# Memory keys and cross-attention queries of an encoder block: two heads at once, high half of the weights with both halves of the activations in one matmul

## The chip, the cores and the metric

The kernel runs on one core of a Trainium2 chip. The metric is the device time in microseconds of one launch; three runs of the kernel before gave 1122.85, 1123.02 and 1123.64 us. Engines: TensorE (PE; its weight loads PEld), VectorE (DVE), ScalarE (ACT), GpSimd (POOL) and SyncE (SP), which here issues the transfers.

## The reference

One encoder block in float32, 256 tokens of width 2048. A mixer of two attention groups is followed by LN1; then cross-attention over 256 memory tokens with four heads of 128, LN2, and an MLP with squared ReLU, LN3. The part that matters here:

```
def memory_cross_attention(h, mem_n, w_q_mem, w_kv_mem, w_o_mem):
    q = (h @ w_q_mem).reshape(b, s, MEM_HEADS, MEM_HEAD_DIM)
    kv = (mem_n @ w_kv_mem).reshape(b, m, 2, MEM_HEADS, MEM_HEAD_DIM)
    k, v = kv[:, :, 0], kv[:, :, 1]
    scores = jnp.einsum('bqhd,bmhd->bhqm', q, k) * (MEM_HEAD_DIM ** -0.5)
    probs = jax.nn.softmax(scores, axis=-1)
    o = jnp.einsum('bhqm,bmhd->bqhd', probs, v).reshape(b, s, MEM_WIDTH)
    return o @ w_o_mem

    x = layer_norm(ALPHA * x + mix, ln1_g[l], ln1_b[l])
    mem_n = layer_norm(mem, mem_ln_g[l], mem_ln_b[l])
    xa = memory_cross_attention(x, mem_n, w_q_mem[l], w_kv_mem[l], w_o_mem[l])
    x = layer_norm(ALPHA * x + xa, ln2_g[l], ln2_b[l])
```

## The kernel before, in words

Every float32 factor is held as a high and a low part (`split`, lines 77 to 84: ScalarE rounds the high part, VectorE subtracts it from the source for the low one). A product is the sum of three matmuls: high by high, high by low, low by high. Activations stand transposed, one block of 128 rows of the contraction beside the next, each as 256 columns of high parts and 256 of low parts.

Weights come as 1 MB transfers into one of three raw buffers (`Stream.next`, line 121). Each raw tile makes two pairs `w_hi`, `w_lo` of 1024 columns, and there are four such pairs. A raw buffer is free again when VectorE has made the second low part from it. A pool of seven temporaries of 512 columns (`tmp_tile`) serves the layer norms, the softmax and the gains and biases; four PSUM banks (`acc`) hold the projections, four more (`att`) the transposes and scores.

In the stage at hand, from 292 us on, TensorE computes for each of four heads the memory keys `km` (`mem_k`, line 613; 16 blocks of 128 rows, `cols_mm`, lines 183 to 187: three matmuls of 256 columns for a block), then the queries `qm` from the normalized activations `x1t` (`mem_q`, line 644; two heads per call), scores and softmax of heads in turn (`softmax`, line 322), the memory values `vm` (line 677, eight halves of weights from four loads, 12 matmuls of 512 columns for a half), the probabilities times values (`values`) and the output projection `w_om`. Beside the keys, the pieces of LN1 are done: `x1t` is transposed on TensorE (line 534, `turn`), scaled on ScalarE (line 542), split on both. Beside the queries the residual gets LN1's gains and biases: `residual` loads a row of 512 values of `ln1_g` or `ln1_b`, broadcast to all partitions, into a temporary (line 561), and VectorE multiplies or adds it to the two blocks of the residual (line 565). After that four halves of the first MLP weights are prepared in a large tile `wide_0` (line 668) from two loads of `w_mi`.

The order of instructions on each engine is chosen by a scheduler from the program's dependences at build time; on the chip each engine then works strictly in that order. Loads share SP's one queue.

The MLP uses `cols_wide` (line 189): for several accumulators of 512 columns, the high weights meet the 512 columns of both activation halves in one matmul, and the low weights meet the 256 high columns in another; `hidden` (line 706) later adds the two halves of the accumulator.

Of the kernel before, what the change touches and what calls it, by code (L numbers as in the profile page):

```python
# [14 lines left out]
AF = mybir.ActivationFunctionType  # L15
ALU = mybir.AluOpType
AX = mybir.AxisListType

P = 128
S = 256  # L20
D = 2048
KT = D // P
# [4 lines left out]
HM = 4  # L27
# [4 lines left out]
SC_A = float(DH) ** -0.5  # L32
# [6 lines left out]
def encoder_kernel(ctx: ExitStack, tc: tile.TileContext, t, out):  # L39
    nc = tc.nc  # L40
# [18 lines left out]
    def f(ap):  # L59
        return ap.bitcast(F32)  # L60

    def acc_tile():
        return psA.tile([P, 512], F32, tag="acc", name="acc")
# [10 lines left out]
    def pin(ins, pinned):  # L74
        return tc.keep_in_program_order(ins) if pinned else ins

    def split(hi, lo, src, scale=None, pinned=False):
        if scale is None:
            pin(nc.scalar.activation(hi, src, AF.Copy), pinned)  # L79
            return pin(nc.vector.tensor_tensor(out=lo, in0=src, in1=f(hi), op=ALU.subtract), pinned)  # L80
        else:
            nc.scalar.activation(hi, src, AF.Copy, scale=scale)
            nc.vector.scalar_tensor_tensor(
                out=lo, in0=src, scalar=scale, in1=f(hi), op0=ALU.mult, op1=ALU.subtract)
# [11 lines left out]
    def pump(n=1):  # L96

        for _ in range(n):
            if side:
                side.popleft()()  # L100
# [82 lines left out]
    def cols_mm(ps, hi, lo, xt, k, nk):  # L183

        nc.tensor.matmul(ps, hi, xt[:, k, 0:S], start=k == 0, stop=False)  # L185
        nc.tensor.matmul(ps, hi, xt[:, k, S:2 * S], start=False, stop=False)  # L186
        nc.tensor.matmul(ps, lo, xt[:, k, 0:S], start=False, stop=k == nk - 1)  # L187
# [244 lines left out]
    ps = proj_tokens(Stream(t["w_ka"]), xt, KT, KVA * DH)  # L432
# [3 lines left out]
    ps = proj_tokens(Stream(t["w_vkr"]), xt, KT, KVA * DH + ROPE)  # L436
    for b in range(NB):
# [3 lines left out]
        a, c, e = krn[:, 0:64], krn[:, 64:128], krn[:, 256:512]  # L441
        nc.vector.tensor_tensor(out=a, in0=v, in1=krt[:, 0, b, :], op=ALU.mult)
        for i in range(2):
            j = 1 - i
            nc.vector.tensor_tensor(out=c[:, i * 32:(i + 1) * 32], in0=v[:, j * 32:(j + 1) * 32],
                                    in1=krt[:, 1, b, i * 32:(i + 1) * 32], op=ALU.mult)
        nc.gpsimd.memset(e, 0.0)
        for par in range(2):
            dst = e[:, par * P:(par + 1) * P].rearrange("p (i g c) -> p i g c", g=2, c=32)
            nc.vector.tensor_tensor(  # L450
                out=dst[:, :, par, :], in0=a.rearrange("p (i c) -> p i c", c=32),
                in1=c.rearrange("p (i c) -> p i c", c=32), op=ALU.add)
# [25 lines left out]
    for n in range(2):  # L478
        ps = proj_tokens(s_vb, ckv, RANK // P, 512)
# [97 lines left out]
    def big3(name):  # L577
        return big.tile([P, 8192], F32R, tag="big", name=name).rearrange("p (k c) -> p k c", c=512)
# [17 lines left out]
    memt = big3("memt")  # L596
# [13 lines left out]
    km = midp.tile([P, 2048], F32R, tag="mid", name="km").rearrange("p (h c) -> p h c", c=512)  # L610
    s_km = Stream(t["w_km"])

    def mem_k(h):
        ps = acc_tile()[:, :S]
        for half in range(2):
            hi, lo = s_km.next()
            for j in range(8):
                c = slice(j * P, (j + 1) * P)
                cols_mm(ps, hi[:, c], lo[:, c], memt, half * 8 + j, KT)
        split(km[:, h, 0:S], km[:, h, S:2 * S], ps)  # L620

    x1t = big3("x1t")
    side.extend(norm_transposed(res_chunk, sts, 1, x1t))
# [4 lines left out]
    qm = attC[:, 2048:4096].rearrange("p (h c) -> p h c", c=512)  # L628
    om = attC[:, 4096:6144].rearrange("p (h c) -> p h c", c=512)

    def together(nexts, xt_, mm, outs):

        n = len(outs)
        for k in range(0, KT, 8 // n):
            hi, lo = nexts(k)
            for j in range(8 // n):
                for i in range(n):
                    c = slice((j * n + i) * P, (j * n + i + 1) * P)
                    mm(outs[i], hi[:, c], lo[:, c], xt_, k + j, KT)

    s_qm = Stream(t["w_qm"], beside=2)
    wide0 = []

    def mem_q(g):
        outs = [acc_tile()[:, :S] for _ in range(2)]
        together(lambda k: s_qm.next(), x1t, cols_mm, outs)
        for j in range(2):
            h = 2 * g + j
            split(qm[:, h, 0:S], qm[:, h, S:2 * S], outs[j], SC_A)

    def mem_scores(h):
        pt = attC[:, 6144 + (h - 2) * 1024:6144 + (h - 1) * 1024] if h >= 2 else None
# [4 lines left out]
               om, h)  # L657

    s_km.beside = 2
    for h in range(HM):  # L660
        mem_k(h)
    pump(len(side))
    side.extend(residual("ln1"))
    mem_q(0)
# [12 lines left out]
    ps = proj_tokens(Stream(t["w_vm"]), memt, KT, 512)  # L677
# [9 lines left out]
    for n in range(4):  # L687
        ps = proj_tokens(s_om, om, HM, 512, by_block=n == 3)
# [48 lines left out]
    for c in range(NCH):  # L737
# [7 lines left out]
        for n in range(4):  # L745
            tiles = att_tile if n >= 2 else acc_tile
            if c == NCH - 1 and n == 3:
                wide_w = [big.tile([P, 8192], F32R, tag="big", name=f"w{i}") for i in range(2)] + [None]
                ps = proj_tokens(None, ht, CH, 512, by_block=True, wide=last_weights, tiles=tiles)
            else:  # L750
                ps = proj_tokens(s_mo, ht, CH, 512, by_block=False, tiles=tiles)
# [13 lines left out]
    for b in range(NB):  # L765
# [10 lines left out]
        for i, c in enumerate(cols):  # L776
            if i + 1 < len(cols):
                shift(cols[i + 1])
            pin(nc.vector.scalar_tensor_tensor(
                out=res[b][:, c], in0=res[b][:, c], scalar=r, in1=b3[:, c],  # L780
# [4 lines left out]
def _rows(w, kt, cols):  # L785

    k, n = w.shape
    u = w.reshape(k // (kt * P), kt, P, n // cols, cols)
    return np.ascontiguousarray(u.transpose(3, 0, 2, 1, 4)).reshape(-1, P, kt * cols)
# [17 lines left out]
def _layout(i):  # L807
    f32 = np.float32
    a = {}
    x = np.asarray(i["x"])[0]  # L810
    a["x"] = x
    a["xT"] = np.ascontiguousarray(x.T.reshape(4, 4, P, S).transpose(0, 2, 1, 3)).reshape(4, P, 4 * S)
    a["mem"] = np.asarray(i["mem"])[0]
    w = np.asarray(i["w_in"])[0]
    qa, ka, va, cq, ckv, kr = np.split(w, np.cumsum([1024, 256, 256, 512, 512]), axis=1)
    a["w_qa"] = _rows(_pairs(qa, DH), 4, 512)
    a["w_ka"] = _rows(_pairs(ka, DH), 8, 256)
    a["w_vkr"] = _rows(np.concatenate([va, _pairs(kr, ROPE)], axis=1), 4, 320)
    a["w_cq"] = _rows(cq, 4, 512)
    a["w_ckv"] = _rows(ckv, 4, 512)  # L820
    gains = []
    for n in ("g_qa", "g_ka"):
        g = _pairs(np.asarray(i[n])[0], DH)
        gains += [g, g[DH // 2:], g[:DH // 2]]
    a["g_qk"] = np.concatenate(gains)
    a["g_cq"], a["g_ckv"] = np.asarray(i["g_cq"])[0], np.asarray(i["g_ckv"])[0]
    uq = np.asarray(i["w_uq"])[0].reshape(RANK, HB, DH + ROPE)
    ukv = np.asarray(i["w_ukv"])[0].reshape(RANK, HB, 2 * DH)

    def cols(m):  # L830
        return m.reshape(4, P, P).transpose(1, 0, 2).reshape(P, 512)
    halves = []
    for p in range(4):
        if p % 2 == 0:
            for pp in (p, p + 1):
                r = _pairs(uq[:, 2 * pp:2 * pp + 2, DH:], ROPE).reshape(RANK, 2, 2, 32)
                halves.append(cols(np.ascontiguousarray(r.transpose(0, 2, 1, 3)).reshape(RANK, P)))
        halves += [cols(uq[:, 2 * p + j, :DH]) for j in range(2)]
        halves += [cols(ukv[:, 2 * p + j, :DH]) for j in range(2)]
    a["w_b"] = np.ascontiguousarray(  # L840
        np.stack(halves).reshape(5, 4, P, 512).transpose(0, 2, 1, 3)).reshape(5, P, 2048)
    a["w_vb"] = _rows(np.ascontiguousarray(ukv[:, :, DH:]).reshape(RANK, HB * DH), 4, 512)
    wo = np.asarray(i["w_out"])[0]
    a["w_out"] = np.concatenate([_rows(wo[:1024], 4, 512), _rows(wo[1024:], 4, 512)])
    kv = np.asarray(i["w_kv_mem"])[0]
    a["w_km"] = _rows(kv[:, :512], 16, P)
    a["w_vm"] = _rows(kv[:, 512:], 4, 512)
    a["w_qm"] = _rows(np.asarray(i["w_q_mem"])[0], 8, 256)
    a["w_om"] = _rows(np.asarray(i["w_o_mem"])[0], 4, 512)
    mi = np.asarray(i["w_mlp_in"])[0]  # L850
    a["w_mi"] = _rows(mi, 4, 512)
    mo = np.asarray(i["w_mlp_out"])[0]
    a["w_mo"] = np.concatenate([_rows(mo[c * CH * P:(c + 1) * CH * P], 4, 512) for c in range(NCH)])
    for n in ("ln1", "ln2", "ln3", "mem_ln"):
        for s in "gb":
            a[f"{n}_{s}"] = np.asarray(i[f"{n}_{s}"])[0]

    a["norm_rows"] = np.ascontiguousarray(np.stack(
        [[a[f"{n}_{s}"].reshape(KT, P) for s in "gb"] for n in ("mem_ln", "ln1", "ln2")]
    ).transpose(3, 0, 1, 2))  # L860

    ang = _angles(DH)
    c, s = np.cos(ang).astype(f32), np.sin(ang).astype(f32)
    cc, ss = np.concatenate([c, c], 1), np.concatenate([-s, s], 1)

    def nat(m):
        return np.ascontiguousarray(m.reshape(NB, P, -1).transpose(1, 0, 2)).reshape(P, -1)
    a["rope_a"] = np.concatenate([nat(cc), nat(ss)], axis=1)
    ang = _angles(ROPE)
    c, s = np.cos(ang).astype(f32), np.sin(ang).astype(f32)  # L870
    cc, ss = np.concatenate([c, c], 1), np.concatenate([-s, s], 1)
    a["rope_kr"] = np.concatenate([nat(cc), nat(ss)], axis=1).reshape(P, 2, NB, ROPE)
    ct, st = c.T, s.T
    a["rope_qr"] = np.ascontiguousarray(
        np.stack([np.concatenate([ct] * 4), np.concatenate([-st, -st, st, st])], axis=1))
    a["rope_qr"] = (a["rope_qr"] * f32(SC_B)).astype(f32)
    return a
# [18 lines left out]
```

## Time and profile before

| | us |
|---|---|
| median of three runs | 1123.02 |
| profiled execution | 1123.25 |
| its span | 1121.4 |
| TensorE busy | 1105.5 (99%) |
| VectorE busy | 729.0 (65%) |
| ScalarE busy | 537.0 (48%) |

The profiled execution is one run with the hardware profiler; its span is the time from its first to its last instruction, and the mean granted clock of TensorE in it is 0.998 of full speed. Busy shares are averages over stages with different limits. A timeline row gives the start in microseconds from the start of the span, the duration, the engine, the line of the code, the operation and its tiles; a matmul's duration is longer than the distance to the next one, since they are pipelined, so their cost is read from starts. For waits, an arrow names who released the waiting instruction.

### The profile page before, as it was taken

What the parts mean: (1) busy time and instruction counts of PE and PEld (TensorE: products, weight loads), DVE (VectorE), ACT (ScalarE), POOL (GpSimd) and SP (SyncE); (2) the same over time, 40 slices, a digit from 0 to 9 for tenths busy, and PEclk for the clock granted to TensorE, in tenths of its full rate; (3) what the DMA queues carried; (4) which work ended last, traced back from release to release, by engine and by line L of the source; (5) the groups of instructions that cost most, each with busy time, mean ns of one, the idle gap of its engine ahead of it and who ended that gap; (6) DMA issues with size and microseconds to landing.
All of it is one profiled execution on the core that took longest, in us unless ns stands there. A gap on an engine that the chain in (4) does not pass through costs nothing.

```text
span 1121.4 us, 15079 instructions
## 1 busy us (share of the span) xinstructions
PE 1105.5 (99%) x6004; PEld 954.2 (85%) x6004; DVE 729.0 (65%) x1036; ACT 537.0 (48%) x778; POOL 38.2 (3%) x45
## 2 busy tenths in 40 slices
PE   9999999999999989999999999999999999999996
PEld 6988899888998878888888888888888888888885
DVE  5878677687788677854545565555556454665575
ACT  6555565546576344543344454334444333544440
POOL 1402000000100000000000000000000000000000
PEclk9999999999999999999999999999999999999999
DMA  9664454476467426655555555555555555555562
GB/s 336 224 225 151 150 188 150 151 240 239 162 224 262 150 75 225 204 205 193 188 189 189 188 186 192 195 198 177 208 188 188 193 188 188 188 188 188 191 259 76
DMA packets 37942, 215.85 MB, mean 192 GB/s; under 512 B 4336, under 2 KB 5232, under 8 KB 14192
## 3 DMA queue, kind: packets, MB, share of 16 engines
q1 hardware_dynamic: 37872, 214.89, 54.6%
q8 instruction: 47, 0.77, 0.3%
q14 instruction: 23, 0.19, 0.1%
HBM read 212.78 MB, written 2.10 MB: 192 GB/s over the span
## 4 chain that ended last, share of the span: by engine, by line
PE 96%; DMA 2%; DVE 1%; ACT 0%; issue 0%; SPq 0%; POOL 0%; DVEq 0%; ACTq 0%
PE acc L146 12%; PE acc L145 12%; PE acc L147 12%; PE acc L194 11%; PE att L194 11%; PE att L147 6%; PE att L145 6%; PE att L146 6%; PE acc L199 5%; PE att L199 5%; PE acc L187 2%; PE acc L185 2%; PE acc L186 2%; PE att L534 1%; PE att L349 1%; DMA raw<-in_w_ka 1%
## 5 line engine op out<-in xcount | busy, mean ns | idle before, releaser
L80 DVE TENSOR_TENSOR w_lo<-raw,w_hi 128x1024 fp32r<-128x1024 f32 (+2 forms) x374 | 444.6, 1193 | 327.4 <-ACT w_hi L79 326.3
L79 ACT ACTIVATE w_hi<-raw 128x1024 fp32r<-128x1024 f32 (+2 forms) x374 | 386.5, 1036 | 459.0 <-PE acc L147 171.0
L194 PE MATMUL att<-x2t,w_hi 128*128 128x512 f32 x512 | 139.6, 394 | 0.0
L194 PE MATMUL acc<-x2t,w_hi 128*128 128x512 f32 x480 | 130.9, 394 | 0.0
L145 PE MATMUL acc<-w_hi,ht 128*128 128x512 f32 x256 | 99.6, 389 | 0.0
L146 PE MATMUL acc<-w_lo,ht 128*128 128x512 f32 x256 | 99.6, 389 | 0.0
L147 PE MATMUL acc<-w_hi,ht 128*128 128x512 f32 x256 | 99.6, 389 | 0.0
L194 PEld LDWEIGHTS att<-x2t,w_hi 128*128 128x128 f32 x512 | 88.1, 189 | 12.3
L194 PEld LDWEIGHTS acc<-x2t,w_hi 128*128 128x128 f32 x480 | 82.5, 189 | 11.5
L146 PE MATMUL att<-w_lo,ht 128*128 128x512 f32 x224 | 87.1, 389 | 0.0
L147 PE MATMUL att<-w_hi,ht 128*128 128x512 f32 x224 | 87.1, 389 | 0.0
L145 PE MATMUL att<-w_hi,ht 128*128 128x512 f32 x224 | 87.0, 389 | 0.0
L199 PEld LDWEIGHTS att<-x2t,w_lo 128*128 128x128 f32 x512 | 77.5, 189 | 10.2
L199 PEld LDWEIGHTS acc<-x2t,w_lo 128*128 128x128 f32 x480 | 72.6, 189 | 9.5
L199 PE MATMUL att<-x2t,w_lo 128*128 128x256 f32 x512 | 80.2, 281 | 0.0
L199 PE MATMUL acc<-x2t,w_lo 128*128 128x256 f32 x480 | 75.1, 281 | 0.0
L146 PE MATMUL acc<-w_lo,xt 128*128 128x512 f32 (+2 forms) x192 | 69.5, 363 | 0.2 <-DVE w_lo L80 0.2
L147 PE MATMUL acc<-w_hi,xt 128*128 128x512 f32 (+2 forms) x192 | 69.1, 361 | 0.0
L145 PE MATMUL acc<-w_hi,xt 128*128 128x512 f32 (+2 forms) x192 | 66.1, 364 | 1.0 <-ACT w_hi L79 1.0
L147 PEld LDWEIGHTS acc<-w_hi,ht 128*128 128x128 f32 x256 | 48.0, 188 | 10.0
L145 PEld LDWEIGHTS acc<-w_hi,ht 128*128 128x128 f32 x256 | 48.0, 188 | 10.0
L146 PEld LDWEIGHTS acc<-w_lo,ht 128*128 128x128 f32 x256 | 48.0, 188 | 10.0
(221 smaller groups left out, 1738.1 us busy)
## 6 DMA issues: line engine op xcount, KB each, us to landing
raw<-in_w_mi SPq DMA_DIRECT2D x64, 1024.0 KB, 4.8
raw<-in_w_mo SPq DMA_DIRECT2D x64, 1024.0 KB, 4.8
raw<-in_w_out SPq DMA_DIRECT2D x16, 1024.0 KB, 4.9
raw<-in_w_b SPq DMA_DIRECT2D x5, 1024.0 KB, 4.8
raw<-in_w_qa SPq DMA_DIRECT2D x16, 256.0 KB, 5.4
raw<-in_w_qa SPq DMA_DIRECT2D x4, 1024.0 KB, 4.9
raw<-in_w_ckv SPq DMA_DIRECT2D x4, 1024.0 KB, 5.1
raw<-in_w_cq SPq DMA_DIRECT2D x4, 1024.0 KB, 4.8
```

What stands on the lines that cost most here:

```text
L79: pin(nc.scalar.activation(hi, src, AF.Copy), pinned)
L80: return pin(nc.vector.tensor_tensor(out=lo, in0=src, in1=f(hi), op=ALU.subtract), pinned)
L145: nc.tensor.matmul(ps, ah, bh, start=start, stop=False)
L146: nc.tensor.matmul(ps, ah, bl, start=False, stop=False)
L147: nc.tensor.matmul(ps, al, bh, start=False, stop=stop)
L185: nc.tensor.matmul(ps, hi, xt[:, k, 0:S], start=k == 0, stop=False)
L186: nc.tensor.matmul(ps, hi, xt[:, k, S:2 * S], start=False, stop=False)
L187: nc.tensor.matmul(ps, lo, xt[:, k, 0:S], start=False, stop=k == nk - 1)
L194: nc.tensor.matmul(ps, hi[:, i * P:(i + 1) * P], xt[:, k, :], start=k == 0, stop=k == nk - 1)
L199: nc.tensor.matmul(ps[:, 0:S], lo[:, i * P:(i + 1) * P], xt[:, k, 0:S], start=False, stop=False)
L349: nc.tensor.transpose(pp[:, st * S + b * P:st * S + b * P + P], ev[:, b, st * P:(st + 1) * P], ident)
L534: nc.tensor.transpose(ps[:, o:o + P], x(b, k // 4)[:, (k % 4 + j) * P:(k % 4 + j + 1) * P], ident)
```

## The change

The weights of the memory keys are laid out for two heads (256 columns of eight blocks in a raw tile instead of 128 columns of 16). Both `mem_k` and `mem_q` now take two heads and two accumulators of 512 columns, and call `cols_wide`: one matmul of 512 columns with the high weights and one of 256 with the low weights for a head and block, instead of three of 256. The new `halves_sum` then has ScalarE copy the second half of an accumulator into a temporary and VectorE add the first half to it; the split of keys or queries works on that sum instead of PSUM. `together` is gone. Below line 640 the new file's line numbers are 5 higher.

```diff
-    def mem_k(h):
-        ps = acc_tile()[:, :S]
-        for half in range(2):
+    def halves_sum(ps):
+
+        tt = tmp_tile()
+        lo, h = tt[:, 0:S], tt[:, S:2 * S]
+        nc.scalar.activation(lo, ps[:, S:2 * S], AF.Copy)
+        nc.vector.tensor_tensor(out=h, in0=ps[:, 0:S], in1=lo, op=ALU.add)
+        return h
+
+    def mem_k(g):
+
+        outs = [acc_tile() for _ in range(2)]
+        for k in range(0, KT, 4):
             hi, lo = s_km.next()
-            for j in range(8):
-                c = slice(j * P, (j + 1) * P)
-                cols_mm(ps, hi[:, c], lo[:, c], memt, half * 8 + j, KT)
-        split(km[:, h, 0:S], km[:, h, S:2 * S], ps)
+            for j in range(4):
+                c = slice(j * S, (j + 1) * S)
+                cols_wide(outs, hi[:, c], lo[:, c], memt, k + j, KT)
+        for j in range(2):
+            h = 2 * g + j
+            split(km[:, h, 0:S], km[:, h, S:2 * S], halves_sum(outs[j]))
...
     def mem_q(g):
-        outs = [acc_tile()[:, :S] for _ in range(2)]
-        together(lambda k: s_qm.next(), x1t, cols_mm, outs)
+        outs = [acc_tile() for _ in range(2)]
+        for k in range(0, KT, 4):
+            hi, lo = s_qm.next()
+            for j in range(4):
+                c = slice(j * S, (j + 1) * S)
+                cols_wide(outs, hi[:, c], lo[:, c], x1t, k + j, KT)
         for j in range(2):
             h = 2 * g + j
-            split(qm[:, h, 0:S], qm[:, h, S:2 * S], outs[j], SC_A)
+            split(qm[:, h, 0:S], qm[:, h, S:2 * S], halves_sum(outs[j]), SC_A)
...
-    for h in range(HM):
-        mem_k(h)
+    for g in range(HM // 2):
+        mem_k(g)
...
-    a["w_km"] = _rows(kv[:, :512], 16, P)
+    a["w_km"] = _rows(kv[:, :512], 8, 256)
```

The scheduler orders the stage anew. Up to its start, and again from about 410 us (the first MLP group), every engine's order is the old one. Three places in between:

The queue of SP, from the last loads of the queries' weights (`in_w_qm`) to the third load of the values' (`in_w_vm`); `in_ln1_g` and `in_ln1_b` are LN1's rows, `in_w_mi` the first MLP weights. Before:

```order
L133 DMA raw_3508<-in_w_qm 128x2048
L561 DMA tmp_3376<-in_ln1_g 128x512
L561 DMA tmp_3378<-in_ln1_b 128x512
L133 DMA raw_3574<-in_w_qm 128x2048
L561 DMA tmp_3442<-in_ln1_g 128x512
L561 DMA tmp_3444<-in_ln1_b 128x512
L561 DMA tmp_3514<-in_ln1_g 128x512
L561 DMA tmp_3516<-in_ln1_b 128x512
L133 DMA raw_3745<-in_w_vm 128x2048
L561 DMA tmp_3580<-in_ln1_g 128x512
L561 DMA tmp_3582<-in_ln1_b 128x512
L133 DMA raw_3751<-in_w_mi 128x2048
```

And in the changed kernel, where `tmp_3324` is the buffer of a key's sum before:

```order
L133 DMA raw_3480<-in_w_qm 128x2048
L133 DMA raw_3641<-in_w_vm 128x2048
L561 DMA tmp_3324<-in_ln1_g 128x512
L561 DMA tmp_3326<-in_ln1_b 128x512
L561 DMA tmp_3374<-in_ln1_g 128x512
L561 DMA tmp_3376<-in_ln1_b 128x512
L133 DMA raw_3647<-in_w_mi 128x2048
L133 DMA raw_3681<-in_w_vm 128x2048
L561 DMA tmp_3436<-in_ln1_g 128x512
L561 DMA tmp_3438<-in_ln1_b 128x512
L561 DMA tmp_3486<-in_ln1_g 128x512
L561 DMA tmp_3488<-in_ln1_b 128x512
```

The first row load has moved behind the last load of the queries' weights and the first of the values'; the last four rows stand behind the second load of the values'.

VectorE where the first MLP tile is made: in the kernel before, after the last gains and biases (`tmp_3582`), with the query splits (L83) and the softmax' maxima (L333):

```order
L565 TENSOR_TENSOR res1_1488<-res1_1488,tmp_3582 128x512
L80 TENSOR_TENSOR w_lo_3748<-raw_3745,w_hi_3747 128x1024
L83 SCALAR_TENSOR_TENSOR attC_3035<-acc_3369,attC_3035 128x256
L80 TENSOR_TENSOR w_lo_3768<-raw_3745,w_hi_3767 128x1024
L80 TENSOR_TENSOR w_lo_3788<-raw_3785,w_hi_3787 128x1024
L83 SCALAR_TENSOR_TENSOR attC_3035<-acc_3506,attC_3035 128x256
L333 TENSOR_REDUCE nm_3652<-att_3645 128x2
L333 TENSOR_REDUCE nm_3669<-att_3662 128x2
L80 TENSOR_TENSOR w_lo_3808<-raw_3785,w_hi_3807 128x1024
L83 SCALAR_TENSOR_TENSOR attC_3035<-acc_3507,attC_3035 128x256
L80 TENSOR_TENSOR wide_0_3644<-raw_3751,wide_0_3644 128x1024 x2
```

In the changed kernel, with the halves' sums (L618):

```order
L80 TENSOR_TENSOR w_lo_3684<-raw_3681,w_hi_3683 128x1024
L618 TENSOR_TENSOR tmp_3530<-acc_3428,tmp_3530 128x256
L565 TENSOR_TENSOR res0_1487<-res0_1487,tmp_3438 128x512
L618 TENSOR_TENSOR tmp_3535<-acc_3429,tmp_3535 128x256
L565 TENSOR_TENSOR res1_1488<-res1_1488,tmp_3438 128x512
L565 TENSOR_TENSOR res0_1487<-res0_1487,tmp_3486 128x512
L565 TENSOR_TENSOR res1_1488<-res1_1488,tmp_3486 128x512
L80 TENSOR_TENSOR wide_0_3540<-raw_3647,wide_0_3540 128x1024
L333 TENSOR_REDUCE nm_3548<-att_3541 128x2
L333 TENSOR_REDUCE nm_3565<-att_3558 128x2
L80 TENSOR_TENSOR wide_0_3540<-raw_3647,wide_0_3540 128x1024
```

The multiply-adds of the third and fourth columns' rows now stand ahead of the first MLP tile, whose second half frees the raw buffer that the third load of the values' weights takes.

TensorE at the start of the queries. Before, transposes stood between single matmuls:

```order
L534 MATMUL att_3223<-ident_88,res0_1487 128x128
L534 MATMUL att_3223<-ident_88,res1_1488 128x128
L185 MATMUL acc_3307<-memt_2555,w_hi_3338 128x256
L186 MATMUL acc_3307<-memt_2555,w_hi_3338 128x256
L534 MATMUL att_3261<-ident_88,res0_1487 128x128
L534 MATMUL att_3261<-ident_88,res1_1488 128x128
L187 MATMUL acc_3307<-memt_2555,w_lo_3339 128x256
L185 MATMUL acc_3368<-x1t_3022,w_hi_3372 128x256
```

In the changed kernel:

```order
L534 MATMUL att_3228<-ident_88,res1_1488 128x128
L534 MATMUL att_3238<-ident_88,res0_1487 128x128
L534 MATMUL att_3238<-ident_88,res1_1488 128x128
L534 MATMUL att_3152<-ident_88,res0_1487 128x128
L534 MATMUL att_3152<-ident_88,res1_1488 128x128
L194 MATMUL acc_3316<-x1t_3022,w_hi_3320 128x512
L199 MATMUL acc_3316<-x1t_3022,w_lo_3321 128x256
L194 MATMUL acc_3316<-x1t_3022,w_hi_3320 128x512
```

The last transposes now stand in one group of eight directly ahead of the first query matmul, whose accumulator `acc_3316` takes the bank of the first key pair's `acc_3036`.

## Rows read from the trace of the kernel before

**Rows 1.** Chain that ended last: share of the span by engine.
```profile
PE 96%; DMA 2%; DVE 1%; ACT 0%; issue 0%; SPq 0%; POOL 0%; DVEq 0%; ACTq 0%
```

**Rows 2.** Windows: length, busy (count) of PE, PEld, DVE, ACT, POOL; clock, DMA share, GB/s.
```profile
285.00:345.00 60.00, 59.99 (x492) 59.24 (x491) 49.08 (x73) 37.54 (x58) 2.91 (x2) 1.00 0.64 211
315.00:340.00 25.00, 25.00 (x211) 25.00 (x211) 23.12 (x33) 14.22 (x22) 0.00 (x0) 1.00 0.77 242
```

**Rows 3.** Waits of PE over the run: us in total, times, longest.
```profile
PE acc L145 <- ACT w_hi L79: 1.0, 2, 0.5
```

**Rows 4.** Timeline of PE, memory queries: start, us, operation; first and last of 42.
```profile
337.39 0.28 PE L185 MATMUL acc<-x1t,w_hi 128*128 128x256 f32 x1
...
342.31 0.28 PE L187 MATMUL acc<-x1t,w_lo 128*128 128x256 f32 x1
```

**Rows 5.** Timeline of PE, MLP: starts of two groups, six groups apart.
```profile
414.25 1.09 PE L194 MATMUL acc<-x2t,w_hi 128*128 128x512 f32 x4
...
422.68 0.40 PE L194 MATMUL acc<-x2t,w_hi 128*128 128x512 f32 x1
```

**Rows 6.** Timeline of PE: two transposes, a matmul between these rows left out.
```profile
317.34 0.38 PE L534 MATMUL att<-ident,res 128*128 128x128 f32 x2
...
317.68 0.28 PE L186 MATMUL acc<-memt,w_hi 128*128 128x256 f32 x1
```

**Rows 7.** Groups on ACT, 292 to 342: count | busy, mean ns | idle before.
```profile
L79 ACT ACTIVATE w_hi<-raw 128x1024 fp32r<-128x1024 f32 x18 | 18.9, 1059 | 17.3 <-PE acc L186 14.1 <-DMA raw<-in_w_vm 3.2
L542 ACT ACTIVATE tmp<-att,gbt 128x256 f32<-128x256 f32 x16 | 8.2, 568 | 0.9 <-PE att L534 0.9
L79 ACT ACTIVATE x1t<-tmp 128x512 fp32r<-128x512 f32 x8 | 5.0, 631 | 0.0
L79 ACT ACTIVATE km<-acc 128x256 fp32r<-128x256 f32 x4 | 1.5, 372 | 0.0
```

**Rows 8.** Groups on DVE, 292 to 342.
```profile
L565 DVE TENSOR_TENSOR res<-res,tmp 128x512 f32<-128x512 f32 x16 | 10.3, 686 | 1.4 <-DMA tmp<-in_ln_g 1.1 <-DMA tmp<-in_ln_b 0.2
...
L80 DVE TENSOR_TENSOR km<-acc,km 128x256 fp32r<-128x256 f32 x4 | 1.7, 419 | 0.0
```

**Rows 9.** Timeline of DVE; in brackets the idle time before and its releaser.
```profile
314.70 0.42 DVE L80 TENSOR_TENSOR km<-acc,km 128x256 fp32r<-128x256 f32 x1
315.03 0.68 DVE L80 TENSOR_TENSOR x1t<-tmp,x1t 128x512 fp32r<-128x512 f32 x1
...
323.09 1.29 DVE L565 TENSOR_TENSOR res<-res,tmp 128x512 f32<-128x512 f32 x2 [1.13 <-DMA tmp<-in_ln_g]
...
351.90 1.22 DVE L80 TENSOR_TENSOR w_lo<-raw,w_hi 128x1024 fp32r<-128x1024 f32 x1
```

**Rows 10.** Timeline of SP: issues of transfers.
```profile
312.36 0.33 SPq L561 DMA_DIRECT2D tmp<-in_ln_g  x1
...
321.65 0.33 SPq L133 DMA_DIRECT2D raw<-in_w_vm  x1
...
345.56 0.33 SPq L133 DMA_DIRECT2D raw<-in_w_vm  x1
```

**Rows 11.** Tile view of the temporaries' loads, 305 to 345, eight loads.
```profile
DMA to landing us min/median/max: 3.1/5.2/7.3
```

**Rows 12.** DMA view of the loads issued at 321.65 and 335.58.
```profile
raw<-in_w_vm SPq DMA_DIRECT2D x1, 1024.0 KB, 7.3
raw<-in_w_vm SPq DMA_DIRECT2D x1, 1024.0 KB, 4.9
```

**Rows 13.** Timeline of PE: memory values' first and 47th matmul; attention's end.
```profile
343.39 0.40 PE L145 MATMUL acc<-w_hi,memt 128*128 128x512 f32 x1
...
353.85 0.39 PE L146 MATMUL acc<-w_lo,memt 128*128 128x512 f32 x1
...
371.36 0.40 PE L364 MATMUL att<-attC 128*128 128x256 f32 x2
371.87 0.50 PE L145 MATMUL acc<-w_hi,attC 128*128 128x512 f32 x1
```

More of the change, by code (lines that the diff above doesn't have):

```diff
@@ L629, in encoder_kernel @@
     om = attC[:, 4096:6144].rearrange("p (h c) -> p h c", c=512)
[L631 to L639, printed above, removed]
     s_qm = Stream(t["w_qm"], beside=2)
```

## Prediction

> **What bounds the kernel now.** I read the chain of waits first: TensorE holds 96% of it [rows 1], so a change counts by what it does to TensorE's stream, and other engines only by making it wait. The stretch table, for the 60 us in which memory keys and queries are computed, then shows TensorE without a pause at full granted clock, VectorE busy for 49.08 us and ScalarE for 37.54 [rows 2]. TensorE's waits over the whole run contain one group for weights' high halves, 1.0 us in two pieces [rows 3]; nothing in this stage. So the stage can gain only by less TensorE work, and can lose by any delay of weights beyond the slack they have. The slack is read further down, and decides my forecast.
>
> **Less TensorE work.** The stage has 2 × 64 pairs of one head and one block of 128 input rows. Each had three matmuls of 256 columns and gets one of 512 and one of 256. The old ones start every (342.31 − 337.39)/41 = 0.120 us, 0.360 a pair [rows 4]. The new pair runs in the MLP already: groups of four and four follow each other, and six such groups take 422.68 − 414.25 = 8.43, so 0.351 a pair [rows 5]. Gain: 128 × 0.009 = 1.15 us.
>
> [...]
>
> The 32 transposes of this stage stood in 17 groups between matmuls and stand in 11 now. [...] From the count I take 0.3 us. Without any wait TensorE is thus 1.4 us earlier: the 51st matmul of the memory values (first with the fifth half's low part), which in the old order without the interposed scores would stand at 343.39 + 50 × 0.2274 = 354.8, with (353.85 − 343.39)/46 = 0.2274 a matmul [rows 13], comes at 353.4.
>
> **Work added.** Eight accumulators get a ScalarE copy and a VectorE add of 256 columns. The same shapes last 0.37 and 0.42 us [rows 7, 8]; successive instructions overlap by some 0.1 us (314.70 + 0.42 against 315.03, [rows 9]), so the engines lose 0.27 and 0.33: 2.1 and 2.6 us in all. The new sums live in tiles of the shared pool of seven temporaries, from copy to the split's low half.
>
> **Bank wait at the first queries.** Their accumulator reuses the bank of the first key pair, which is free only after its add on VectorE. TensorE gets there at 317.3: the keys' start near 292.2, 64 pairs of 0.351, and about 2.6 for the transposes among and behind them. VectorE, in program order, first makes a low half whose high half ScalarE can deliver, from transposes that TensorE passes at 311.2, at 311.6 + 4 × 0.46 + 0.52 + 0.95 = 314.9 (four short activations, one split, itself; rows 7 less the overlap), then three x1t splits, then the add: 315.0 + 1.14 + 1.8 + 0.42 = 318.4. Wait about 1.1 us. Alone this leaves −1.4 + 1.1 = −0.3.
>
> **Gains and biases of LN1 come late.** This is the step that matters. On the one DMA queue of SP the first row load was issued at 312.36 [rows 10], because its temporary was free. Now its buffer is that of the second key's sum, released by that key's low split. On ScalarE there stand before this split's high part, from 311.6, nine short activations, four splits of 512, two high halves and five copies or splits of 256: 9 × 0.568 + 4 × 0.631 + 2 × 1.059 + 5 × 0.372 − 20 × 0.11 = 9.4 us [rows 7], 321.0; the low part is done at 321.5. And the 1 MB load of values that stood behind these rows is now ahead of them (order of SP). Old row loads landed 3.1, 5.2, 7.3 us after issue (least, median, most) [rows 11]; I take 4.7 here, so 326.2. VectorE, strictly in program order, could be there at 325.7: little lost at this point. From 326.2 it has eight multiply-adds at 0.60, three x1t and one key split, and three low halves: 8 × 0.60 + 3 × 0.60 + 0.33 + 3 × 1.14 = 10.4, so 336.6 [rows 8, 9].
>
> The last of these low halves frees the raw buffer of the second values load, and the third g row stands right behind this load on SP. It is issued at about 337. The 1 MB takes 4.9 [rows 12] to 341.6, and the row lands at 342.2 to 343.4. VectorE, with two low halves, two adds and two query splits between (3.6 us), is at that row's multiply by 340.2 and stands 2 to 3 us. In the trace of before there was such a stand of 1.13 us, too [rows 9], but with slack behind it.
>
> Then come six multiply-adds, two adds, a low half, two halves of the first MLP tile and two maxima: 6 × 0.60 + 0.66 + 1.14 + 2 × 1.14 + 2 × 0.60 = 8.9 (order of VectorE), from 342.5: 351.4. The second half of that MLP tile is what frees the raw buffer of the third values load. This load was issued at 345.56 [rows 10] and is now issued near 351.5. Landing 4.9 later, 356.4; high half on ScalarE 1.06, low half on VectorE 1.22 [rows 7, 8]: 358.7. TensorE wants it at 353.4 (or 354.5 after the bank wait). Before, that low half started at 351.90 [rows 9] and was done at 353.0. TensorE stands 4 to 5 us, and the fifth half's first low matmul is at 358.8 against 354.8: **+4.0**. The gain and the bank wait are swallowed by this: whatever comes before a late load no longer counts.
>
> **After the values.** The splits of the last two heads' probabilities now stand on ScalarE behind the values' own splits and a further high half. From the last value matmul ScalarE has four splits of 512, that half and a short split: 4 × 0.52 + 0.96 + 0.27 = 3.3 us, TensorE eight transposes and twelve matmuls, about 0.7 + 1.4. The first output matmul waits some 1.3 us, where the old gap was 371.87 − 371.36 − 2 × 0.12 = 0.27 [rows 13]; interludes made fewer give 0.5 back. Together +0.5, between −0.5 (splits in time) and +1.4. From the first MLP group on, all engines' orders are the old ones, so nothing is given back: its loads have slack, but a TensorE at 99% can't run faster.
>
> **Sum.** 4.0 + 0.5 = 4.5 on the profiled execution's 1123.25, which is 0.2 above the median of the runs, 1123.02. I predict 1127.3.
>
> **Rivals.**
> - *Rows land in time.* If the first rows take the 3.1 us of the shortest, VectorE doesn't stand at 326 or 342, ends the MLP tile some 3 us earlier, and the fifth half is ready at 355.8: +1.0, with the end +0.3, so 1124.5. For it: seven of eight old loads gave VectorE no long wait. Against it: they are issued behind 1 MB.
> - *Only less work, loads hidden.* All loads keep their slack: −1.4, and at best −0.5 after the values: 1121.4; with the bank wait 1122.5. This ends on the faster side. It decides if VectorE gets through the MLP tile before 346, 5 us sooner than I have it. For it: VectorE is idle for 10.9 of the 60 us, more than the 2.6 added. Against it: between 315 and 340, where the work is added, it is busy for 23.1 of 25 [rows 2].
> - *Loads queue.* Rows at 7.3 us, and the third values load at 7.3, as the one issued at 321.65 [rows 10, 12]: VectorE stands 1.5 longer, the load 2.4 longer, and 1131 comes out.
>
> **How the numbers follow.** A difference of under 0.2% (2.2 us) I count as no change, which is what a measurement here can tell. Late loads as worked out, 0.55; loads queue, 0.10; rows in time, 0.17; hidden, 0.18, of which a third beyond 0.2% faster. So slower: 0.55 × 0.95 + 0.10 + a sixth of the rival "in time" = 0.65; faster 0.07; same 0.28. Range: from the hidden case with the bank wait, 1122.2, to 1130.5.
>
> **What would show it.** In the changed profile: pairs at 0.351 us between 292 and 340, with SP's first LN1 row issued near 321 and the third near 337; VectorE waiting for in_ln1_g twice; the third values load issued at 351 instead of 345.6; a TensorE wait of several microseconds on the fifth half of the values' weights, put down to w_hi or w_lo; and after 410 us both streams parallel. I am wrong if the third values load is issued before 348, or if TensorE shows no wait over 2 us in 345 to 360.

## The result and the profile after

The changed kernel took 1128.38 us (median of six runs, 1127.63 to 1130.0) against 1122.93 before: ratio 1.0050, interval 1.0037 to 1.0063, so slower by 5.45 us; forecast was 1127.3. The profiled execution is the slowest of the six: 1130.0 us with a span of 1128.2, 6.75 above the profiled one before. The account below is of that execution; the median is 1.6 lower.

**The chain forecast, link by link.** First the matmuls. Timeline of TensorE at the memory keys, two heads' groups of two and two, nine groups from the first to the last row ([rows 4] is the old form):

```profile
292.88 0.63 PE L194 MATMUL acc<-memt,w_hi 128*128 128x512 f32 x2
293.35 0.39 PE L199 MATMUL acc<-memt,w_lo 128*128 128x256 f32 x2
...
299.16 0.63 PE L194 MATMUL acc<-memt,w_hi 128*128 128x512 f32 x2
```

6.28/18 = 0.349 us a pair, against 0.360 before. Then SP's issues, to be held against [rows 10]:

```profile
320.05 0.33 SPq L133 DMA_DIRECT2D raw<-in_w_vm  x1
321.97 0.33 SPq L561 DMA_DIRECT2D tmp<-in_ln_g  x1
...
336.68 0.33 SPq L133 DMA_DIRECT2D raw<-in_w_vm  x1
337.06 0.43 SPq L561 DMA_DIRECT2D tmp<-in_ln_g  x1
...
351.14 1.46 SPq L133 DMA_DIRECT2D raw<-in_w_vm  x2
```

The first row of LN1 was issued 9.6 us later than before, the third stands behind the second values load, and the third values load came at 351.14 instead of 345.56. VectorE between the second and the third, with its idle time in brackets, as in [rows 9]:

```profile
339.68 0.76 DVE L83 SCALAR_TENSOR_TENSOR attC<-tmp,attC 128x256 fp32r<-128x256 f32 x2
342.14 1.29 DVE L565 TENSOR_TENSOR res<-res,tmp 128x512 f32<-128x512 f32 x2 [1.71 <-DMA tmp<-in_ln_g]
343.36 1.22 DVE L80 TENSOR_TENSOR w_lo<-raw,w_hi 128x1024 fp32r<-128x1024 f32 x1
...
349.90 1.22 DVE L80 TENSOR_TENSOR wide<-raw,wide 128x1024 fp32r<-128x1024 f32 x1
```

It stands 1.71 us for the row and ends the second half of the MLP tile at 351.1; at that moment SP issues the load. TensorE's waits in the whole run, and the two places in its timeline that belong to them:

```profile
PE acc L145 <- ACT w_hi L79: 3.4, 3, 2.3
PE att L534 <- DVE res L521: 2.6, 2, 1.4
PE acc L110 <- DVE ones L103: 1.1, 1, 1.1
PE acc L194 <- DVE tmp L618: 1.0, 1, 1.0
PE acc L146 <- DVE w_lo L80: 0.8, 2, 0.5
PE acc L145 <- ACT attC L79: 0.6, 1, 0.6
```
```profile
318.61 0.50 PE L194 MATMUL acc<-x1t,w_hi 128*128 128x512 f32 x1 [0.95 <-DVE tmp L618]
...
357.17 0.74 PE L145 MATMUL acc<-w_hi,memt 128*128 128x512 f32 x2 [2.31 <-ACT w_hi L79]
358.43 0.79 PE L146 MATMUL acc<-w_lo,memt 128*128 128x512 f32 x1 [0.53 <-DVE w_lo L80]
359.02 0.63 PE L147 MATMUL acc<-w_hi,memt 128*128 128x512 f32 x1
359.45 0.63 PE L146 MATMUL acc<-w_lo,memt 128*128 128x512 f32 x1
```

The bank wait is there (0.95 us), and the fifth half's first low matmul starts at 358.43, where the old order would have had it at 354.8: +3.7.

**What the forecast did not have.** After the pause, matmuls of 512 columns start every 0.43 us (359.02, 359.45) instead of 0.2274 [rows 13]. Windows of the changed kernel (columns as in [rows 2]) show why: the granted clock, the first figure after the counts, is 0.50.

```profile
358.40:363.70 5.30, 5.27 (x12) 4.02 (x13) 4.52 (x7) 2.42 (x3) 0.00 (x0) 0.50 0.87 301
363.70:370.00 6.30, 6.30 (x37) 5.67 (x36) 4.31 (x8) 3.65 (x9) 0.00 (x0) 0.93 0.60 237
```

The twelve matmuls from 358.43 to 363.72 run at it: 5.3 us instead of 12 × 0.2274 = 2.7.

**The sum.** Up to the fifth half +3.7. From there to the last matmul of the output projection, 358.43 to 400.63 is 42.2 us; before it would be 354.76 (the 354.8 above) to 393.82, 39.06. Of these 3.1 us the low clock has some 2.9 (an estimate: the twelve matmuls above lose 2.6, the window behind them is at 0.93; the run with the wait filled, below, gives 2.85), waits behind the values the rest. From that last matmul to the first of the MLP both kernels need 8.47 us, and from there to the end of the span 719.1, although the order is not wholly the old one there, as stated ahead: three pairs of transposes stand elsewhere among the first MLP matmuls, up to about 416. So all of the 6.8 us arise between 292 and 401; nothing is given back.

### The profile page after: what moved, and what is told of

It is laid out like the page before. It is cut to its first block, busy times and chain, and to the rows that moved or that the text cites. A ratio compares the mean times of both kernels' runs of the same rounds, so it can differ in the third digit from the quotient of the medians.

```text
span 1128.2 us, 14834 instructions
## 1 busy us (share of the span) xinstructions
PE 1108.2 (98%) x5876; PEld 949.5 (84%) x5876; DVE 731.9 (65%) x1044; ACT 539.9 (48%) x786; POOL 37.4 (3%) x45
## 4 chain that ended last, share of the span: by engine, by line
PE 93%; DMA 3%; DVE 3%; ACT 1%; SPq 0%; issue 0%; POOL 0%; DVEq 0%; ACTq 0%
PE acc L194 12%; PE acc L146 12%; PE acc L147 12%; PE acc L145 12%; PE att L194 11%; PE acc L199 6%; PE att L145 6%; PE att L146 6%; PE att L147 6%; PE att L199 5%; PE acc L187 1%; PE acc L186 1%; PE acc L185 1%; PE att L534 1%; PE att L349 1%; DMA raw<-in_w_ka 1%
```

## The experiments

Theory L is the one forecast: sums in the shared temporaries make LN1's rows late, VectorE stands and works in an order that makes the third values load late. Rival W: the eight copies and adds, and the bank wait, cost by themselves. Theory C: the pause costs clock on top. Each ratio is against runs of the kernel before taken with that run; their medians are 1123.10 to 1123.21, against 1122.93 above, so a difference in microseconds from the changed kernel is good to some 0.3.

**Sums in a buffer of their own.** The place where the new pool pressure arises is taken away:

```diff
-        tt = tmp_tile()
-        lo, h = tt[:, 0:S], tt[:, S:2 * S]
-        nc.scalar.activation(lo, ps[:, S:2 * S], AF.Copy)
-        nc.vector.tensor_tensor(out=h, in0=ps[:, 0:S], in1=lo, op=ALU.add)
+        h = qrt[:, j, :]
+        nc.scalar.activation(h, ps[:, S:2 * S], AF.Copy)
+        nc.vector.tensor_tensor(out=h, in0=ps[:, 0:S], in1=h, op=ALU.add)
```

> The changed kernel, but the eight sums are made in a buffer of their own (the rotary table of an earlier stage, no longer used) and not in the pool of seven temporaries; copy, add and splits are unchanged. Theory L (LN1's row loads wait for temporaries held by the sums, VectorE stands behind them, the third values load is late): the first LN1 row is issued before 316, the third values load before 347.5, no TensorE wait over 1 us in 345 to 360, granted clock 1.00 there, and 1121.3 to 1123.0 us. Rival W (the added copies and adds themselves, and the bank wait at the first queries, are the cost): still 1126 or more.

Measured: 1125.22 us, ratio 1.0018 (1.0009 to 1.0027). The first row was issued at 317.05 and the third values load at 348.31, both about 1 us later than expected; no wait for the fifth half is left, and the granted clock from 345 to 360 is 1.00. So 3.2 us of the loss hung on the shared temporaries. But the forecast of 1123 or less missed. TensorE of this kernel has a new wait:

```profile
326.33 0.50 PE L199 MATMUL acc<-x1t,w_lo 128*128 128x256 f32 x2 [2.05 <-DVE w_lo L80]
```

And VectorE ahead of it:

```profile
320.76 1.29 DVE L565 TENSOR_TENSOR res<-res,tmp 128x512 f32<-128x512 f32 x2 [0.73 <-DMA tmp<-in_ln_g]
321.97 0.76 DVE L80 TENSOR_TENSOR km<-qrt,km 128x256 fp32r<-128x256 f32 x2
322.64 2.49 DVE L565 TENSOR_TENSOR res<-res,tmp 128x512 f32<-128x512 f32 x4
325.05 1.22 DVE L80 TENSOR_TENSOR w_lo<-raw,w_hi 128x1024 fp32r<-128x1024 f32 x1
```

With the rows there early, six multiply-adds and a stand of 0.73 us come ahead of a low half of query weights that TensorE wants at 324.3. The same kind of work hurts at another place, and the clock adds to it: it is 0.74 from 325 to 330.

**The MLP tile later.** The other link is cut: the four prepared MLP halves go behind the memory values, so that they hold no raw buffer that the values want.

```diff
-    side.extend([lambda u=u: s_mi0.next(wide_0[:, u, 0, :], wide_0[:, u, 1, :]) for u in range(4)])
...
     ps = proj_tokens(Stream(t["w_vm"]), memt, KT, 512)
...
+    side.extend([lambda u=u: s_mi0.next(wide_0[:, u, 0, :], wide_0[:, u, 1, :]) for u in range(4)])
     for h in range(HM):
```

> The changed kernel, sums in the shared temporaries, but the four prepared halves of the first MLP weights are put into the program behind the memory values, so that the third values load no longer waits for a raw buffer that they hold. Theory L: LN1 rows are issued as late as in the changed kernel (near 322 and 337) and VectorE still stands over 1 us for one, yet the third values load is issued before 347 and TensorE has no wait over 1 us for the fifth half: 1122 to 1124.5 us. Rival W: 1126 or more, since copies, adds and the bank wait stay.

Measured: 1124.3 us, ratio 1.0010 (1.0001 to 1.0019); the intervals of this and of the changed kernel are apart. SP in this run:

```profile
332.62 4.41 SPq L133 DMA_DIRECT2D raw<-in_w_vm  x2
337.08 0.43 SPq L561 DMA_DIRECT2D tmp<-in_ln_g  x1
...
339.80 0.33 SPq L133 DMA_DIRECT2D raw<-in_w_vm  x1
```

The third values load is the second of the pair in the first row, near 337, while LN1's rows are as late as in the changed kernel. VectorE's stand for a row is 0.59 us, not over 1 as expected; copies, adds and the bank wait (0.95) are all still there. 4.1 us of 5.45 are gone, the low clock after the pause among them: the late load is the cause of the bulk.

The same move on the kernel before:

> The kernel before with the same move of the four prepared MLP halves behind the memory values: the control for the move. Theory L: the loads had slack, so within 1 us of before, 1122 to 1124; if the move by itself speeds up or slows the kernel by more than 1 us, the run with the late tile has to be read against this one.

1123.04 us, ratio 0.9998 (0.9989 to 1.0007): the move alone does nothing.

**No sums at all.** The splits read the accumulators' first halves.

```diff
-            split(km[:, h, 0:S], km[:, h, S:2 * S], halves_sum(outs[j]))
+            split(km[:, h, 0:S], km[:, h, S:2 * S], outs[j][:, :S])
...
-            split(qm[:, h, 0:S], qm[:, h, S:2 * S], halves_sum(outs[j]), SC_A)
+            split(qm[:, h, 0:S], qm[:, h, S:2 * S], outs[j][:, :S], SC_A)
```

> The changed kernel without the eight copies and adds: the splits read the first half of each accumulator alone, so that the product of high weights with low activations is left out. Both theories: the work of TensorE alone remains, 1120.9 to 1122.3 us; theory L says that this is within 1 us of the kernel with sums in a buffer of their own, rival W that it is 4 us or more below it.

1124.1 us, ratio 1.0008 (0.9999 to 1.0017): above what both theories gave. Against sums in their own buffer it is 1.1 us lower, and the intervals overlap: the copies and adds cost about a microsecond and, by the ends of the intervals, not four. (The bank wait of W is in neither of the two runs.) The fewer matmuls alone did not speed the kernel up either. TensorE again waited, 1.92 us on a low half at 325.31, with five multiply-adds and two waits for their rows (0.77 and 1.02) ahead of it on VectorE.

**The wait filled.** Ten matmuls on constants directly ahead of the fifth half:

```diff
-    ps = proj_tokens(Stream(t["w_vm"]), memt, KT, 512)
+    ps = proj_tokens(Stream(t["w_vm"]), memt, KT, 512, before=lambda k: busy(10) if k == 8 else None)
```

> The changed kernel with ten matmuls on a constant tile, 512 columns each, whose result nobody reads, put on TensorE directly ahead of the fifth half of the memory values, where it stood for 2.3 us. The data still comes when it came. Theory C (after a pause of over 2 us the granted clock falls to half for some 6 us, and this is worth about 2.9 of the loss): the wait is filled, the granted clock in 355 to 365 stays 1.00, and the time is 1125.0 to 1126.5 us. Without theory C: 1128 us or, if the dummies overrun the wait, up to 1129.

In the profiled execution the theory holds. TensorE:

```profile
354.19 2.33 PE L110 MATMUL acc<-ones 128*128 128x512 bf16 x10
356.60 0.73 PE L145 MATMUL acc<-w_hi,memt 128*128 128x512 f32 x2
357.86 0.50 PE L146 MATMUL acc<-w_lo,memt 128*128 128x512 f32 x1 [0.53 <-DVE w_lo L80]
358.19 0.40 PE L147 MATMUL acc<-w_hi,memt 128*128 128x512 f32 x1
358.43 0.39 PE L146 MATMUL acc<-w_lo,memt 128*128 128x512 f32 x1
```

The data come as late as ever (357.86), matmuls then start every 0.23 us, the clock from 358 to 363 is 1.00, and from here to the output projection's last matmul at 397.21 it takes 39.35 us instead of 42.2: 2.85 us. The median says less: 1127.52 us (ratio 1.0026 to 1.0052), 0.9 below the changed kernel and above what I expected, with overlapping intervals. The two profiled executions are also the slowest of six and the fastest of five. So the clock's price is shown for the profiled execution; how much of it an average execution pays is open. The mean granted clock of whole executions points the same way, 0.993 to 0.995 in the six of the changed kernel and 0.995 or 0.996 in these five, but it holds other stretches too.

**Gains and biases spread.** Sums in their own buffer, and one of LN1's pieces instead of two for each half of the query weights:

```diff
-    s_qm = Stream(t["w_qm"], beside=2)
+    s_qm = Stream(t["w_qm"])
```

> Sums in a buffer of their own, and LN1's gain and bias pieces taken one instead of two per half of query weights, so that half of them go beside the memory values. Theory L extended (whatever VectorE has in its order ahead of a weight's low half, multiply-adds above all, delays TensorE; with this out of the way only the saved matmuls remain): no TensorE wait over 0.7 us between 292 and 375, clock 1.00, 1121.0 to 1122.5 us. Rival W (the eight copies and adds cost by themselves): 1123.5 or more.

> The kernel before with the gain and bias pieces taken one instead of two per half of query weights: the control for that move. Both theories: 1122.3 to 1123.6 us, no change, since the old kernel had no wait there. If the move itself brings something it shows here.

Both missed: 1128.31 (ratio 1.0034 to 1.0060) and, for the control, 1127.33 us (1.0021 to 1.0048). The first wait did not go: TensorE of the spread kernel still stands 2.08 us on a low half of query weights at 326.75, behind six multiply-adds. The other multiply-adds now stand beside the values, ahead of the low parts of probabilities and values, and TensorE waits at the attention's end as well:

```profile
374.09 0.39 PE L364 MATMUL att<-pt,attC 128*128 128x256 f32 x1 [2.08 <-DVE attC L80]
```

The control waits 1.83 us at the same place. Since the move costs 4 us in the old kernel by itself, the pair says nothing on W; it shows a second time that these multiply-adds hurt wherever they precede a low part.

**Both links cut.**

> Sums in a buffer of their own and the prepared MLP halves behind the memory values. Theory L extended: the third values load is early, but the stand at 326 (multiply-adds ahead of a low half of query weights) stays as in the run with sums of their own: TensorE waits about 2 us there, half clock after it, 1124 to 1125.5 us. If the late tile also moves the multiply-adds: 1121.5 to 1123.

1125.01 us (ratio 1.0012 to 1.0030), as expected: the wait at 325.74 is 2.17 us. Its granted clock there stayed 1.00, where the kernel with sums of their own had 0.74 from 325 to 330 after a wait of 2.05: such a pause does not lower the clock every time. First the kernel with sums of their own, then this one (columns as in [rows 2]):

```profile
325.00:330.00 5.00, 3.67 (x15) 3.19 (x16) 4.86 (x8) 2.20 (x5) 0.00 (x0) 0.74 0.55 179
325.00:330.00 5.00, 4.26 (x24) 3.75 (x25) 5.00 (x8) 2.28 (x4) 0.00 (x0) 1.00 0.91 185
```

**The multiply-adds on GpSimd.**

```diff
-            nc.vector.tensor_tensor(out=r, in0=r, in1=rows[w], op=ALU.mult if w == "g" else ALU.add)
+            eng = nc.gpsimd if name == "ln1" else nc.vector
+            eng.tensor_tensor(out=r, in0=r, in1=rows[w], op=ALU.mult if w == "g" else ALU.add)
```

> Sums in a buffer of their own, and LN1's sixteen multiply-adds on GpSimd (idle here) instead of VectorE. Theory L extended (the multiply-adds ahead of the low halves in VectorE's order make TensorE wait at 326, not the copies and adds): the 2 us wait on w_lo at 326 is gone, no wait over 0.7 us from 292 to 370, clock 1.00 in 320 to 345, 1121.5 to 1123 us. Rival W (copies and adds): still 1124 or more. A GpSimd instruction of this size lasted 1.95 us in the trace of before, so sixteen take 31 us, from 320 to 351: the output projection at 371 should not wait for them.

> The kernel before with LN1's sixteen multiply-adds on GpSimd: the control. Both theories: the old kernel had no wait on them, 1122.5 to 1123.5 us, no change; a slowdown would be GpSimd's own.

1126.41 us (ratio 1.0017 to 1.0040) and, for the control, 1124.41 (0.9998 to 1.0016); both expectations on time missed. The wait at 326 is gone, as L says, but VectorE has become slow. Its groups from 320 to 350:

```profile
L80 DVE TENSOR_TENSOR w_lo<-raw,w_hi 128x1024 fp32r<-128x1024 f32 x7 | 14.8, 2137 | 0.5 <-ACT w_hi L79 0.5
...
L618 DVE TENSOR_TENSOR qrt<-acc,qrt 128x256 f32<-128x256 f32 x4 | 1.5, 410 | 0.0
```

A low half lasts 2137 ns instead of the changed kernel's 1218 while GpSimd works for 30 us beside it; the add that reads an accumulator lasts 410, against 417. TensorE now waits 1.58 and 0.68 us for low parts of the queries (342.25 and 343.67), and in the control 1.48 us for a low part of `x1t` (330.35). So the run shows that the multiply-adds on VectorE made the wait at 326; on W the pair says nothing, since the slow VectorE is mixed in. The third values load is issued at 351.61, as late as in the changed kernel, and yet TensorE does not wait for the fifth half; the last experiment shows why.

**One half of the change at a time.** The old code for queries, or for keys:

> Only the memory keys are changed (two heads, wide matmuls, sums in the shared temporaries); the queries are the old ones. Theory L: the order of SP has the LN1 rows behind the first values load as in the changed kernel, all eight of them ahead of the first MLP load, so VectorE's multiply-adds and the third values load come late too: 1124 to 1128 us. Rival: if the queries carry the loss, 1122 to 1123.5.

> Only the queries are changed; the keys are the old ones, one head at a time. Theory L: the first two LN1 rows are issued ahead of the last query weights as before, so the first part of the loss is absent: the third values load before 349, 1122 to 1124.5 us. Rival: if the queries carry the loss, 1126 or more.

Keys alone: 1124.7 us, ratio 1.0013 (1.0004 to 1.0022), LN1's first row at 321.41, third values load at 347.85. Queries alone: 1122.5 us, ratio 0.9993 (0.9984 to 1.0002), first row at 312.28, third values load at 349.60, not before 349 as expected, and without a wait of TensorE on the values' weights. Both times are as L expects, its chain only in part: with the keys alone the load is 2.3 us later than before, but TensorE's waits are the bank wait (0.95) and 0.25 us on a low half at 349.61, and its profiled execution, the fastest of ten, is only 0.3 us above the one before; where the median's 1.5 us come from is open. Neither part alone has the loss of the whole, and the queries alone are the best version found, not distinguishable from before.

The queries alone also show what else the wait needs. The transposes (L349) and scores of the last heads are some 2.3 us of TensorE's work (354.31 to 356.61 in the kernel before). They start here in the kernel before, the changed one and this one:

```profile
354.31 0.38 PE L349 MATMUL att<-ident,tmp 128*128 128x128 f32 x2
363.72 0.63 PE L349 MATMUL att<-ident,tmp 128*128 128x128 f32 x2
354.09 0.44 PE L349 MATMUL att<-ident,tmp 128*128 128x128 f32 x2 [0.41 <-DVE tmp L343]
```

In the kernel before, with the queries alone and with GpSimd (356.17) they stand ahead of the fifth half's first low matmul, and TensorE has work while its weights come; the scheduler of the changed kernel put them behind this half. Of the four profiles with a third values load near 350 or later (changed, filled, GpSimd, queries alone) only the two with the scores behind have TensorE short of work there. No run moves these scores alone, and with GpSimd TensorE's other waits also make it come later, so what the old place would give back in the changed kernel is not shown.

## Why the prediction was right, point by point

- *Less TensorE work*: 0.349 a pair against 0.351 forecast; right. No run shows the 0.3 us taken for the fewer groups of transposes: in the trace of before a group of four (at 286.16, the next matmuls at 286.52 and 286.72) costs 286.72 − 286.16 − 0.12 = 0.44 us, twice the 0.22 of a group of two [rows 6]. What is left of it is less than forecast: from the first key matmul to the end of the values' 48th it is 62.57 us (292.13 to 354.70) against 62.12 before (292.19 to 354.31), so apart from the bank wait 0.5 us are saved and not 1.4. Where the rest went is not settled. The late load hides it in the sum.
- *Bank wait*: 0.95 us against 1.1; right, and as forecast it did not count in the end, being ahead of a later load. (Six of the 32 transposes stand behind the first queries, at 322.48 and 323.62; the group of eight is not the last, as stated ahead.)
- *LN1's rows late*: first issue 321.97 against 321.5, second group 337.06 against 337, VectorE's stand 1.71 at 342.14 against 2 to 3 us ending near 342.5; right in place, a little short. VectorE waited for in_ln1_g once, not twice: the first row landed as VectorE got there, which the working had allowed.
- *Third values load*: 351.14 against 351.5; fifth half's low matmul 358.43 against 358.8. Term +3.7 against +4.0. Cutting either link (own buffer, late tile) removes the wait.
- *After the values*: the wait before the output projection was 0.58 us against 1.3; about +0.3 against +0.5 in the sum.
- *Not in the sum*: the half clock after the pause, 2.9 us in the profiled execution. This alone puts that execution at +6.75 instead of near +4; in the median it is smaller, and by how much is not settled. So there is luck in the number: a term is missing, and the range has room for it only because of the rival *loads queue*. The sum itself is 0.2 off: 4.5 on 1123.02 is 1127.5, not 1127.3.
- *Rivals*: rows in time is ruled out by VectorE's stand at 342.14 (the first row landed 4.2 us after its issue), loads hidden by SP's third values load; queueing loads too, since the 1 MB of the third values load took 4.8 us. "Hidden" failed for a reason I had only half: even without the late load the saved 1.2 us did not show. With sums in their own buffer, no sums or both links cut, VectorE's multiply-adds get in front of the next low half; with the late tile alone the bank wait (0.95) and waits behind the values (0.49 and 0.36) remain. A version that gets them out of the way without a new cost was not found.

## What to carry to other kernels

Where one engine is at 99%, ask of a change that saves it work what the helpers do to the buffers: a temporary held a little longer moved a small load, that load stopped an engine that works in order, and this engine freed the buffer of the next large load. What the late weight then costs depends on what TensorE's own order has ahead of it. Follow the program's order and waits from the first moved load to the first weight that comes late; the size of the gain ahead of that point no longer matters. And price a pause of TensorE not only by its length: look at the granted clock behind it.

## What the runs showed of the hardware

After a pause of 2.3 and 0.5 us TensorE ran for 5.3 us at a granted clock of 0.50; filled with matmuls on constants, the same place ran at 1.00. Seven waits of 1.8 to 2.3 us stand in this stage in these runs. Five were followed by a lower clock (a mean over the stretch named, which can hold full clock too): the one above, 2.05 us (sums in their own buffer, 0.74 from 325 to 330), 1.92 (no sums, 0.93 from 320 to 345; two matmuls of 512 columns took 0.86 us at 325.85 and 0.46 at 330.47), 2.08 (spread, 0.81 from 325 to 330) and 1.83 (control of spread, 0.85 from 365 to 375). Two were not: 2.17 us (both links cut, 1.00 from 325 to 330) and the second of the spread kernel, 2.08 (1.00 from 365 to 375 and from 375 to 390). So the length of the pause alone does not decide it.

In the LN2 transposes ahead of the MLP the clock was 0.66 from 405 to 410 in the changed kernel and 1.00 from 398 to 403 before, the same distance behind the projection, with the same 8.47 us from projection to MLP: there TensorE is not what sets the time.

While GpSimd worked beside it, VectorE's subtraction of two 128x1024 operands from SBUF took 2.14 us instead of 1.22, and its add with one operand in PSUM was no slower (0.41 us against 0.42).
